# Encoder layer, output products: an earlier copy on ScalarE, a residual cut in two, two VectorE steps moved behind logits

## The chip, the cores and the metric

The kernel runs on one core of one Trainium2 chip. The metric is device time in microseconds of one execution; of a kernel several executions are timed and the median stands for it. In the profile PE is TensorE, PEld its weight loads, DVE is VectorE, ACT is ScalarE, POOL is GpSimd, and SP is SyncE, which here issues every DMA. Each engine takes its instructions strictly in the order in which the program holds them.

## The reference

One layer over 4096 tokens of 1024 channels, float32:

```
h = rmsnorm(x, pre_norm_g);  proj = h @ w_in                # 1024 -> 2304
q, k, v, g_a, u_p, g_p = split(proj)
a = banded_attention(q, k, v, rel_bias, sink) * silu(g_a)    # 8 heads of 64, 2 KV heads, |i-j| <= 128
p = multiscale_pool(u_p, pool_w, pool_scale) * silu(g_p)     # windows 2, 4, 8, 16
mixed = concat([a, p]) @ w_out                               # 1024 -> 1024
out = x + rmsnorm(mixed, post_norm_g)
```

`banded_attention` takes blocks of 128 queries against the block before, the same and the block after (384 keys). The softmax has a learned sink logit in its denominator. Every float32 operand of a product is carried as a pair of float16 (high and low part, three products for one).

## The kernel before, in words

The first half (to about 515 us) computes pooling, gates and the input projections and keeps some of them in DRAM. The second half, which alone is changed, goes backwards through 32 query blocks `b`, two of them (256 tokens) to a *unit* `u = b // 2`. For a unit it computes k, v and q, then for each block and each half of the heads (`visit(b, half)`) a softmax, then the attention values, and the output product.

A softmax is a chain over four engines: `scores` (PE, line 1272), four `logits` (DVE, line 1295), four `exps` (ACT, line 1306), `denominators` and a reciprocal (DVE, lines 1313 and 1316), four `probs` (ACT, line 1328: the high half `pn`), four `rests` (DVE, line 1336: the low half), and `turn` (SP, line 1345: one DMA that transposes all of it into `pt`). `values` (PE, line 1422) needs `pt` of both halves of a block; within a block it works through half 0 first and then half 1.

The output product of a unit is a 2x2 block product done in seven products instead of eight, named "11", "12", "22", "s1" to "s4" (12 matmuls each, line 1572). They share three PSUM banks 0 to 2 (`acc0` to `acc2`), and partial sums live in two SBUF tiles `mo[0]`, `mo[1]` of a unit (128x1024 float32, one buffer each for all units from 2 on, so unit `u` takes over the buffers of unit `u + 1`). The steps which the change touches:

- `mix_p1`: product "11" into bank 0; `begin` (ACT, line 1590, "COPY mo") copies bank 0 into the upper half of `mo[0]`.
- `mix_p6`: product "s2" into bank 1. `mix_p2`: product "12" is added on top in bank 0, so its first matmul must wait for `begin`. Then `square` (ACT, line 1595, "jkb") and `gain11` (DVE, line 1600) both read bank 0.
- `mix_p3`: product "s4"; it ends `mo[0]` of a unit: `mean` (DVE 1624, POOL 1629), `residual` (DVE, line 1633, "xr": `xr = mo * rs + xr`), `store` (SP, line 1639).

In the loop over odd blocks the order on PE is: "s4" of the unit before, k and v, `values(b+1)`, `scores(b, 1)`, then "22", "11", "s2", "12". The softmax of `(b, 1)` on DVE and ACT so runs beside these four products. The loop goes through this 13 times (units 14 to 2). The last units (2, 1 and 0) are written out one by one behind the loop, with `at_(t, step)`.

The order is a plan written by hand: `due(t, step)` puts a step into a list with a time `t`; the list is sorted by `t` and issued in that order, each engine receiving its own instructions. `t` is no time of the chip, it only sets the order. `pe(us, step)` moves PE's own planned clock on. Waits are set by a framework layer: by data, and a tile that takes over a buffer waits for the last reader of the tile before. Two readers of one PSUM bank on different engines are put one behind the other, in the order of the plan.

Of the kernel before, what the change touches and what calls it, by code (L numbers as in the profile page):

```python
# [19 lines left out]
D = 1024  # L20
# [19 lines left out]
O11, O12, O21, O22, OT1, OT2, OT4, OT3 = range(8)  # L40
# [94 lines left out]
def hybrid_layer(ctx: ExitStack, tc, io, out):  # L135
# [74 lines left out]
    with ExitStack() as actx:  # L210
# [689 lines left out]
        for j in range(4):  # L900
            ld(9.5 + 0.1 * j, wut[:, j], io["w_uT"][j], 0.5, w=[f"wut{j}"])
            z = turn("sq")
            for half in range(2):
                t = U0 + 4 * j + 2 * half
# [338 lines left out]
    def due(t, fn, *args):  # L1243
        plan.append((t, len(plan), fn, args))
# [283 lines left out]
    LO, HI = slice(0, 512), slice(512, D)  # L1528
# [123 lines left out]
    def pe(us, fn, *args):  # L1652

        due(now[0], fn, *args)
        now[0] += us
        return now[0]
# [27 lines left out]
    M = 2.6  # L1684

    def mix_p1(u):
        due(pe(M, product, u, "11", O11, 0) - 0.2, begin, u)

    def mix_p4(u):
        pe(M, product, u, "22", OT4, 2)  # L1690

    def mix_p2(u):
        t = pe(M, product, u, "12", O21, 0, True)
        due(t, square, u, 0, 0, 0)
        due(t + 0.1, gain11, u)

    def mix_p6(u):
        due(pe(M, product, u, "s2", OT2, 1), add, u, (0, HI), (0, HI), 1)
# [8 lines left out]
    def mix_p5(u):  # L1707
        t = pe(M, product, u, "s1", OT1, 1)
        due(t, add, u, (1, HI), (1, HI), 1)
        due(t + 0.7, square, u, 1, 1)  # L1710
        due(t + 1.4, gain, u, 1, HI)
        finish(u, 1, t + 4.0)

    def mix_p3(u):
        t = pe(M, product, u, "s4", O22, 1, True)
        due(t, add, u, (0, HI), (0, HI), 1)
        due(t + 0.7, square, u, 0, 1)
        due(t + 1.4, gain, u, 0, HI)
        finish(u, 0, t + 4.0, 6.4)

    def finish(u, i, t, late=0.0):

        due(t, mean, u, i)
        due(t + 2.0 + late, residual, u, i, slice(0, D))
        due(t + 3.4 + late, store, u, i, slice(0, D))

    u = NU - 1
# [10 lines left out]
    for b in reversed(range(2, NB)):  # L1740
        u = b // 2
# [13 lines left out]
        elif b == NB - 3:  # L1755
            due(free[1], load_wo, OT3)
            mix_p4(u + 1)
            mix_p1(u + 1)
            attend(b + 1, 1)
            visit(b, 1)  # L1760
            due(free[1], load_wo, OT1)
            due(free[1] + 8.0, load_wo, O22)
            do_kv(u - 1, 1)
            mix_p2(u + 1)
            mix_p6(u + 1)
        elif b % 2:
            mix_p3(u + 2)
            do_kv(u - 1)
            attend(b + 1, 0)
            visit(b, 1)  # L1770
            mix_p4(u + 1)
            mix_p1(u + 1)
            mix_p6(u + 1)
            mix_p2(u + 1)
        else:
            do_q(u - 1, 0, 2.0 * (b == NB - 2))
            if b < NB - 2:
                attend(b + 1, 0)
            visit(b, 1)
            do_q(u - 1, 1, 2.0 * (b == NB - 2), int(b < NB - 2))  # L1780
            due(now[0] + 2.1, load_x, u - 3)
            if b == NB - 2:
                attend(b + 1, 1)
            elif b > 2:
                mix_p7(u + 1)
                mix_p5(u + 1)
# [15 lines left out]
    def at_(t, fn, *args):  # L1802
        due(z + t, fn, *args)
# [11 lines left out]
    def cast(th, tw, u, name, f, eng):  # L1815
        at_(th, high, u, name, f)
        at_(tw, low, u, name, f, eng)

    def ending(u, i, tm, tr, split=False):
        at_(tm, mean, u, i)  # L1820
        for n, cs in enumerate((LO, HI) if split else (slice(0, D),)):
            at_(tr + 0.7 * n, residual, u, i, cs)
            at_(tr + 1.3 + 0.7 * n, store, u, i, cs)
# [39 lines left out]
    at_(12.3, square, 2, 0, 1)  # L1863
    at_(11.1, gain, 2, 1, LO, V)
    at_(11.8, gain, 2, 1, HI, V)
    ending(2, 1, 10.9, 12.5)
    at_(38.7, gain, 2, 0, HI, V)
    ending(2, 0, 13.8, 39.4)

# [7 lines left out]
    at_(16.55, sum4, 1)  # L1877
    cast(16.6, 18.9, 1, "s2", a11, V)
    cast(18.0, 18.1, 1, "s3", a21, G)
    at_(17.4, gain11, 1)  # L1880
    at_(17.8, square, 1, 0, 0, 0)
    cast(23.5, 24.2, 1, "s1", a_s1, V)
    at_(23.45, add, 1, (0, HI), (0, HI), 1)
# [115 lines left out]
```

## Time and profile before

| what | value |
|---|---|
| median of 3 runs | 1194.64 us (1194.54 to 1195.63) |
| the profiled execution | 1195.91 us, of which the span of its trace is 1194.10 us |
| PE busy | 1154.7 us, 97% of the span |
| DVE, ACT, POOL busy | 942.1, 702.1, 302.2 us |
| granted TensorE clock, mean | 0.996 |
| PE waiting for the copy of line 1590 | 6.7 us in 12 waits |

A timeline row reads: start (us from the span's start), duration, engine, line, operation, output<-inputs, shape, how many instructions were merged, and in brackets how long the engine sat idle before it and who released it. A row of waits reads: who waited, for whom, total us, number of waits, longest.

### The profile page before, as it was taken

How to read it: one execution, taken by the hardware profiler on the slowest of the kernel's cores; microseconds unless marked ns; L12 is line 12 of the kernel's file. 1: busy time of each engine (PE TensorE's matmuls, PEld its weight loads, DVE VectorE, ACT ScalarE, POOL GpSimd, SP SyncE). 2: the span in 40 equal slices, each digit the busy share in tenths (PEclk: the TensorE clock that was granted, in tenths of full speed). 3: DMA queues.
4: the chain of work that ended last, by engine and by line, in shares of the span. 5: the costliest groups of instructions: out<-in, count | busy, mean ns of one | idle time of the engine just before them, and what ended most of it. 6: DMA issues, size and time to landing. Idle time of an engine off the chain costs nothing. (4 is left out here: it accounts for less than half of the span.)

```text
span 1194.1 us, 33947 instructions
## 1 busy us (share of the span) xinstructions
PE 1154.7 (97%) x14304; PEld 884.4 (74%) x14304; DVE 942.1 (79%) x1866; ACT 702.1 (59%) x1459; POOL 302.2 (25%) x309
## 2 busy tenths in 40 slices
PE   5999999999999999898999999999999999999997
PEld 4998888988888888776667676576666667657643
DVE  6889996867888972567878877887887887788786
ACT  5865555645755541266565675666666567566662
POOL 0002111101101110203324433432542443343231
PEclk9999999999999999999999999999999999999999
DMA  8544587578657573487976876786786687686684
GB/s 315 209 124 151 168 280 242 171 238 261 217 174 251 164 203 109 135 229 177 255 177 139 201 185 128 198 196 164 173 188 177 136 204 187 133 187 164 162 233 124
DMA packets 292441, 224.65 MB, mean 188 GB/s; under 512 B 210704, under 2 KB 251920, under 8 KB 287680
## 3 DMA queue, kind: packets, MB, share of 16 engines
q1 hardware_dynamic: 292288, 222.48, 68.5%
q8 instruction: 112, 1.84, 0.6%
q14 instruction: 41, 0.34, 0.1%
HBM read 113.37 MB, written 60.33 MB: 145 GB/s over the span
## 5 line engine op out<-in xcount | busy, mean ns | idle before, releaser
L634 PEld LDWEIGHTS <-wq 128*128 128x128 f16 x4104 | 401.5, 98 | 52.8 <-issue 2.8
L634 PE MATMUL y<-xt,wq 128*128 128x256 f16 x1512 | 204.2, 273 | 0.9 <-ACT cc L742 0.9
L1336 DVE SCALAR_TENSOR_TENSOR pn<-p,rd,pn 128x384 f16<-128x384 f32 (+1 forms) x256 | 156.7, 654 | 30.5 <-ACT pn L1328 29.9
L1227 PE MATMUL aq<-xb,xb 128*128 128x256 f16 x1024 | 175.1, 275 | 0.0
L1306 ACT ACTIVATE p<-p,nm 128x385 f32<-128x385 f32 (+1 forms) x256 | 152.8, 599 | 33.5 <-DVE nm L1295 28.1
L1572 PE MATMUL ms<-wo,ys 128*128 128x512 f16 x720 | 163.1, 380 | 1.3 <-ACT pn L1328 0.9
L1295 DVE CUSTOM_DVE_ANT_0 p<-s,nt,nsink 128x384 f32<-128x384 f32 (+1 forms) x256 | 155.9, 665 | 1.5 <-PE s L1272 1.3
L1328 ACT ACTIVATE pn<-p,rd 128x384 f16<-128x384 f32 (+1 forms) x256 | 137.7, 598 | 30.7 <-issue 19.5
L1227 PEld LDWEIGHTS <-xb 128*128 128x128 f16 x1280 | 125.7, 98 | 23.7 <-issue 6.7
L1227 PE MATMUL aq<-xb,xt 128*128 128x256 f16 x512 | 140.5, 274 | 0.0
L1572 PEld LDWEIGHTS <-ys 128*128 128x128 f16 x720 | 69.0, 98 | 83.4 <-issue 3.4
L1572 PE MATMUL m<-wo,y 128*128 128x512 f16 x540 | 121.8, 380 | 7.8 <-ACT mo L1590 6.7
L304 POOL TENSOR_TENSOR yt<-yt,sg 128x512 f32<-128x512 f32 (+2 forms) x32 | 48.0, 1499 | 311.4 <-DVE yt L307 300.8
L1572 PEld LDWEIGHTS <-y 128*128 128x128 f16 x540 | 51.4, 98 | 73.2 <-issue 13.1
L1606 POOL TENSOR_TENSOR mo<-mo,gpost 128x512 f32<-128x512 f32 x39 | 63.8, 1636 | 92.9 <-ACT jkb L1595 91.7
L634 PE MATMUL plain<-xb,wq 128*128 128x256 f16 x576 | 68.8, 277 | 3.0 <-ACT xb L446 1.8
L1272 PE MATMUL s<-k_all,q 64*32 64x288 f16 (+8 forms) x3648 | 63.7, 268 | 6.9 <-ACT q L1216 3.9
L1227 PEld LDWEIGHTS <-xt 128*128 128x128 f16 x640 | 62.9, 98 | 8.7
L634 PE MATMUL y<-xb,wq 128*128 128x256 f16 x504 | 68.9, 273 | 0.0
L634 PE MATMUL v<-xb,wq 128*128 128x256 f16 x504 | 68.6, 273 | 0.2 <-DVE cc L304 0.2
L634 PE MATMUL v<-xt,wq 128*128 128x256 f16 x504 | 68.6, 273 | 0.0
L634 PE MATMUL x<-xb,wq 128*128 128x256 f16 x504 | 68.3, 273 | 0.0
(211 smaller groups left out, 1912.2 us busy)
## 6 DMA issues: line engine op xcount, KB each, us to landing
nt<-in_xT SPq DMA_DIRECT2D x28, 512.0 KB, 4.8
x_scr<-xb SPq DMA_DIRECT2D x14, 1024.0 KB, 7.2
xb<-x_scr SPq DMA_DIRECT2D x14, 1024.0 KB, 7.5
xr<-in_x SPq DMA_DIRECT2D x28, 512.0 KB, 4.5
out<-xr SPq DMA_DIRECT2D x28, 512.0 KB, 2.6
xn<-in_x SPq DMA_DIRECT2D x27, 512.0 KB, 4.5
ga_scr<-cc SPq DMA_DIRECT2D x64, 128.0 KB, 2.1
raw<-in_w_out SPq DMA_DIRECT2D x16, 512.0 KB, 5.3
```

Source lines behind the costliest of these rows:

```text
L304: eng.tensor_tensor(out=out, in0=in0, in1=in1, op=op)
L634: nc.tensor.matmul(b[:, s], wq[:, slot[q, op], wv, s, k, :], x[:, xv, k, :], start=(first and k + s + wv + xv == 0), stop=(last and k == H ...
L1227: nc.tensor.matmul(acc, w[:, j, k, :], x[:, kh, v, kt, :], start=(n == 0), stop=(n == 3 * KT - 1),)
L1272: nc.tensor.matmul(s_ps[qs, gg, c0:c1], q_t[u, half][a, qi, jj, tl + 32 * hq : tl + 32 * hq + 32], k_all[a, ki, kc + c0 - s0 : kc + c1 - s ...
L1295: nc.vector.tensor_tensor_reduce(out=p_t[b, half][:, hh, :nk], in0=s_t[jj][:, gg, :nk], in1=bias[:, h, lo : lo + nk], scale=negc[:, h : h ...
L1306: nc.scalar.activation(p[:, hh, : nk + 1], p[:, hh, : nk + 1], AF.Exp, bias=nm_t[b, half][:, hh : hh + 1], scale=-1.0, accum_out=den_t[b, ...
L1328: nc.scalar.activation(prob_view(b, half)[:, 0, i], p_t[b, half][:, i, :nk], AF.Copy, scale=rd_t[b, half][:, i : i + 1],)
L1336: nc.vector.scalar_tensor_tensor(out=pn4[:, 1, i], in0=p_t[b, half][:, i, :nk], scalar=rd_t[b, half][:, i : i + 1], in1=pn4[:, 0, i], op0= ...
L1572: nc.tensor.matmul(z_t[u, tag], y[:, k, yi, :], wo[o][:, wi, k, :], start=(n == 0 and acc is None), stop=(n == 3 * HK - 1), skip_group_che ...
L1606: eng.tensor_tensor(out=mo, in0=mo, in1=gpost[:, cs], op=ALU.mult)
```

## The change

Four edits to the plan, and no change to what is computed. `begin` is due 0.8 earlier. In `mix_p2`, `gain11` comes first and `square` 0.1 behind it. The residual that `mix_p3` ends with is issued as two halves of 512 channels, with the store still one. Among the written-out last units, the residual of block 4 (unit 2, `i = 1`; its store with it) and `gain11` of unit 1 come later.

```
     def mix_p1(u):
-        due(pe(M, product, u, "11", O11, 0) - 0.2, begin, u)
+        due(pe(M, product, u, "11", O11, 0) - 1.0, begin, u)
...
         t = pe(M, product, u, "12", O21, 0, True)
-        due(t, square, u, 0, 0, 0)
-        due(t + 0.1, gain11, u)
+        due(t, gain11, u)
+        due(t + 0.1, square, u, 0, 0, 0)
...
         due(t + 1.4, gain, u, 0, HI)
-        finish(u, 0, t + 4.0, 6.4)
+        due(t + 4.0, mean, u, 0)
+        due(t + 12.4, residual, u, 0, LO)
+        due(t + 13.1, residual, u, 0, HI)
+        due(t + 13.8, store, u, 0, slice(0, D))
...
-    ending(2, 1, 10.9, 12.5)
+    ending(2, 1, 10.9, 19.2)
...
-    at_(17.4, gain11, 1)
+    at_(19.1, gain11, 1)
```

`finish` loses its argument `late`, which no other call used; its planned times are the same as before.

ACT's order at the copy, unit 9, before (`p`, `den`: exponentials; `pn`: probabilities; `m_9`: PSUM bank 0; `ys`, `jkb`: operands and squares of the output product):

```order
L1306 ACTIVATE p_1_11951,den_1_11949<-p_1_11951,nm_1_11948 128x385 [waits DVE_49] x3
L1328 ACTIVATE pn_1_11980<-p_1_11951,rd_1_11950 128x384 [waits DMAHW4_49,DVE_49,Activation_49]
L1590 COPY mo_0_11983<-m_9_11963 128x512 [waits PE_49]
L1328 ACTIVATE pn_1_11980<-p_1_11951,rd_1_11950 128x384 [waits Activation_49]
L1328 ACTIVATE pn_1_11980<-p_1_11951,rd_1_11950 128x384
L1328 ACTIVATE pn_1_11980<-p_1_11951,rd_1_11950 128x384 [waits Activation_49]
L1474 CAST ys_9_12025<-at_11880 128x4x128
L1474 CAST ys_9_12027<-s_9_11931 128x4x128 [waits PE_49]
L1595 ACTIVATE jkb_00_12030,ss_11985<-m_9_11963 128x512
```

And now:

```order
L1306 ACTIVATE p_1_11956,den_1_11954<-p_1_11956,nm_1_11953 128x385 [waits DVE_49] x3
L1590 COPY mo_0_11983<-m_9_11968 128x512 [waits DVE_49,PE_49]
L1328 ACTIVATE pn_1_11989<-p_1_11956,rd_1_11955 128x384 [waits DMAHW4_49,Activation_49]
L1328 ACTIVATE pn_1_11989<-p_1_11956,rd_1_11955 128x384 [waits Activation_49]
L1328 ACTIVATE pn_1_11989<-p_1_11956,rd_1_11955 128x384
L1328 ACTIVATE pn_1_11989<-p_1_11956,rd_1_11955 128x384 [waits Activation_49]
L1474 CAST ys_9_12031<-at_11885 128x4x128
L1474 CAST ys_9_12033<-s_9_11936 128x4x128 [waits PE_49]
L1595 ACTIVATE jkb_00_12133,ss_11985<-m_9_11968 128x512 [waits DVE_49]
```

The copy moved one place, ahead of the first of the four probabilities, and now names a wait for DVE itself: the instruction waited for is the second half of the residual, the last reader of the buffer which `mo[0]` takes over. The square now waits for DVE too, which is `gain11`.

DVE's order at the same place, unit 9, before (ISA: a logits instruction; `xr`: the residual of the unit before):

```order
L1295 ISA p_1_11951,nm_1_11948<-s_5947,nt,nsink,negc 128x384
L1295 ISA nm_1_11948 128x1
L1633 SCALAR_TENSOR_TENSOR xr_11499<-mo_0_11190,rs_0_11788,xr_11499 128x1024 [waits DMAHW3_49,DMAHW1_49,Pool_49]
L1313 TENSOR_SCALAR den_1_11949<-den_1_11949 128x4 [waits Activation_49]
L1316 RECIPROCAL rd_1_11950<-den_1_11949 128x4 [waits DVE_49]
L1336 SCALAR_TENSOR_TENSOR pn_1_11980<-p_1_11951,rd_1_11950,pn_1_11980 128x384 [waits DMAHW4_49,Activation_49]
L1336 SCALAR_TENSOR_TENSOR pn_1_11980<-p_1_11951,rd_1_11950,pn_1_11980 128x384 [waits Activation_49] x3
L1611 TENSOR_TENSOR mo_0_11983<-ms_9_11989,mo_0_11983 128x512 [waits PE_49]
L1600 TENSOR_TENSOR mo_0_11983<-m_9_11963,gpost 128x512 [waits Activation_49]
```

And now:

```order
L1295 ISA p_1_11956,nm_1_11953<-s_5947,nt,nsink,negc 128x384
L1295 ISA nm_1_11953 128x1
L1633 SCALAR_TENSOR_TENSOR xr_11504<-mo_0_11189,rs_0_11793,xr_11504 128x512 [waits DMAHW3_49,DMAHW1_49,Pool_49]
L1313 TENSOR_SCALAR den_1_11954<-den_1_11954 128x4 [waits Activation_49]
L1316 RECIPROCAL rd_1_11955<-den_1_11954 128x4 [waits DVE_49]
L1633 SCALAR_TENSOR_TENSOR xr_11504<-mo_0_11189,rs_0_11793,xr_11504 128x512
L1336 SCALAR_TENSOR_TENSOR pn_1_11989<-p_1_11956,rd_1_11955,pn_1_11989 128x384 [waits DMAHW4_49,DVE_49,Activation_49]
L1336 SCALAR_TENSOR_TENSOR pn_1_11989<-p_1_11956,rd_1_11955,pn_1_11989 128x384 [waits Activation_49] x3
L1611 TENSOR_TENSOR mo_0_11983<-ms_9_11995,mo_0_11983 128x512 [waits DVE_49,PE_49]
L1600 TENSOR_TENSOR mo_0_11983<-m_9_11968,gpost 128x512 [waits PE_49]
```

The residual's second half now stands behind the reciprocal, and `gain11` (line 1600) waits for PE's product "12", where it waited for ACT's square. Its place in the row is the same. This holds for all 13 units of the loop.

DVE's order among the last units, softmax of block 1, half 1, before (`xb<-m_1`: `gain11` of unit 1; `ys_1<-at`: the low part of operand "s2"). The residual of block 4 stood seven instructions ahead of these rows, just ahead of the `gate` of block 2:

```order
L1295 ISA p_1_18618,nm_1_18615<-s_5946,nt,nsink,negc 128x384
L1295 ISA nm_1_18615 128x1
L1600 TENSOR_TENSOR xb_68<-m_1_18407,gpost 128x512 [waits PE_49]
L1295 ISA p_1_18618,nm_1_18615<-s_5947,nt,nsink,negc 128x384
L1295 ISA nm_1_18615 128x1
L1295 ISA p_1_18618,nm_1_18615<-s_5947,nt,nsink,negc 128x384
L1295 ISA nm_1_18615 128x1
L1478 TENSOR_TENSOR ys_1_18622<-at_18171,ys_1_18622 128x4x128 [waits Activation_49]
L1313 TENSOR_SCALAR den_1_18616<-den_1_18616 128x4 [waits Activation_49]
```

And now:

```order
L1295 ISA p_1_18629,nm_1_18626<-s_5947,nt,nsink,negc 128x384
L1295 ISA nm_1_18626 128x1
L1478 TENSOR_TENSOR ys_1_18633<-at_18184,ys_1_18633 128x4x128 [waits Activation_49]
L1600 TENSOR_TENSOR xb_68<-m_1_18420,gpost 128x512 [waits Activation_49]
L1633 SCALAR_TENSOR_TENSOR xr_18237<-mo_1_17925,rs_1_18472,xr_18237 128x1024 [waits DMAHW7_49,Pool_49]
L1313 TENSOR_SCALAR den_1_18627<-den_1_18627 128x4 [waits Activation_49]
```

Both steps now stand between the last logits and the denominators. On SP the store of block 4 moved behind the loads of a gate, of a pooling operand and of a weight, to just ahead of the transpose of block 1, half 1. On PE and POOL nothing moved.

More of the change, by code (lines that the diff above doesn't have):

```diff
@@ L1718, in mix_p3, with finish @@
         due(t + 1.4, gain, u, 0, HI)
-        finish(u, 0, t + 4.0, 6.4)
-    def finish(u, i, t, late=0.0):
+        due(t + 4.0, mean, u, 0)
+        due(t + 12.4, residual, u, 0, LO)
+        due(t + 13.1, residual, u, 0, HI)
+        due(t + 13.8, store, u, 0, slice(0, D))
+    def finish(u, i, t):
         due(t, mean, u, i)
-        due(t + 2.0 + late, residual, u, i, slice(0, D))
-        due(t + 3.4 + late, store, u, i, slice(0, D))
+        due(t + 2.0, residual, u, i, slice(0, D))
+        due(t + 3.4, store, u, i, slice(0, D))
     u = NU - 1
```

## The prediction

> **What bounds the kernel now.** I read the page first, then the waits of PE, then the timeline of each engine around the longest of them.
>
> ```profile
> span 1194.1 us, 33947 instructions
> PE 1154.7 (97%) x14304; PEld 884.4 (74%) x14304; DVE 942.1 (79%) x1866; ACT 702.1 (59%) x1459; POOL 302.2 (25%) x309
> PEclk9999999999999999999999999999999999999999
> ```
>
> PE is the bound, at a granted clock in the top tenth throughout. Only its idle time can be won, so I ask what PE waits for. From 640 us on, and (third row) between 500 and 640 us:
>
> ```profile
> PE m L1572 <- ACT mo L1590: 6.0, 11, 0.6
> PE s L1272 <- DVE nm L1295: 1.1, 1, 1.1
> PE m L1572 <- ACT mo L1590: 0.7, 1, 0.7
> ```
>
> The copy costs PE 6.7 us in 12 listed waits; the loop runs 13 times, and I count 13. The second row is one wait among the last units. Both are what the change touches. One pass (unit 9) on PE, ACT, DVE and POOL:
>
> ```profile
> 810.39 2.75 PE L1572 MATMUL ms<-wo,ys 128*128 128x512 f16 x12
> 813.72 2.75 PE L1572 MATMUL m<-wo,y 128*128 128x512 f16 x12 [0.58 <-ACT mo L1590]
> 810.51 0.60 ACT L1306 ACTIVATE p<-p,nm 128x385 f32<-128x385 f32 x1
> 812.59 0.62 ACT L1328 ACTIVATE pn<-p,rd 128x384 f16<-128x384 f32 x1 [1.38 <-issue]
> 813.11 0.56 ACT L1590 COPY mo<-m 128x512 f32<-128x512 f32 x1
> 813.57 1.63 ACT L1328 ACTIVATE pn<-p,rd 128x384 f16<-128x384 f32 x3
> 810.32 1.89 DVE L1633 SCALAR_TENSOR_TENSOR xr<-mo,rs,xr 128x1024 f32<-128x1024 f32 x1
> 812.13 0.16 DVE L1313 TENSOR_SCALAR den<-den 128x4 f32<-128x4 f32 x1
> 812.33 0.18 DVE L1316 RECIPROCAL rd<-den 128x4 f32<-128x4 f32 x1
> 817.75 0.69 DVE L1600 TENSOR_TENSOR mo<-m,gpost 128x512 f32<-128x512 f32 x1 [1.25 <-ACT jkb L1595]
> 809.86 1.28 POOL L1516 TENSOR_TENSOR yf<-yf,at 128x512 f32<-128x512 f32 x1
> ```
>
> Product "s2" ends at 813.14 and "12" starts at 813.72, 0.61 after the copy started. The copy's data was there long before, since "11" stands ahead of "s2" on PE. It starts late because it stands behind the first probability, which waits for the reciprocal (ends 812.51), which stands on DVE behind the residual.
>
> **The change part by part, against the profiled execution (1195.91 us: span 1194.10 and 1.81 around it; the median, 1194.64, is 1.27 lower).**
>
> *The copy.* ACT is idle from about 811.2 (the exponential above, 0.60, and its accumulator read) to 812.59. If the copy could run there, "12" would follow "s2" at once: the listed 0.58 would go. But the copy now waits for the residual's second half, which is behind the reciprocal. When does that end? Rows for the durations of a residual and of a half, and for what may follow a reciprocal:
>
> ```profile
> 798.75 1.28 DVE L1633 SCALAR_TENSOR_TENSOR xr<-mo,rs,xr 128x1024 f32<-128x1024 f32 x1 [0.36 <-POOL rs L1629]
> 798.81 2.36 POOL L1606 TENSOR_TENSOR mo<-mo,gpost 128x512 f32<-128x512 f32 x1
> 1184.57 0.75 DVE L1633 SCALAR_TENSOR_TENSOR xb<-xb,rs,xb 128x512 f32<-128x512 f32 x1
> 1168.84 0.18 DVE L1316 RECIPROCAL rd<-den 128x4 f32<-128x4 f32 x1
> 1168.93 0.66 DVE L1611 TENSOR_TENSOR xb<-ms,xb 128x512 f32<-128x512 f32 x1
> ```
>
> Undisturbed, a residual takes 1.28. At 810.32 it took 0.61 more, beside a POOL instruction begun 0.46 earlier; at 798.75 it began 0.06 before POOL and POOL was the one that paid (2.36). So the later of the two is held, and here the first half pays the 0.61: 0.75 + 0.61, and, since the next instruction starts 0.08 before the listed end (812.13 against 812.21), the denominators start at 810.32 + 1.28 = 811.60. Reciprocal at 811.80 (0.20 behind, as before), second half at 811.90 (0.09 behind a reciprocal, last two rows), end 812.65, copy at 812.73 (ACT followed DVE by 0.08 before: 812.51 to 812.59). "12" then starts at 812.73 + 0.61 = 813.34: **0.38 earlier**, a third of the wait left. The bounds: nothing (the second half held as well), and 0.58.
>
> *The Trainium skill on that hold.* The page "SBUF — State Buffer", section "SBUF: two separate sides", says that the port pair of VectorE and GpSimd is an exclusive lock for a whole instruction, and that a VectorE instruction with two SBUF inputs blocks fully against it. By that the sum would be the one of the third rival below. The trace agrees on who pays, but not in full: blocked to POOL's end at 811.14, the residual of before would have ended at 812.42, and it ended at 812.21.
>
> *The probabilities behind the copy.* The first starts at 812.73 + 0.46 = 813.19 instead of 812.59, the last at 814.73 instead of 814.59, since the copy is no longer between them. The rests end, and the transpose is issued, 0.14 later, while PE comes 0.38 earlier. What waits for the transpose is the second half of the next `values`:
>
> ```profile
> 815.96 3.64 SPq L1345 DMA_TRANSPOSE pt<-pn  x1
> DMA to landing us min/median/max: 7.2/7.2/7.2
> DMA to landing us min/median/max: 5.5/5.5/5.5
> DMA to landing us min/median/max: 5.4/7.0/8.2
> 822.80 0.25 PE L1422 MATMUL o<-pt,vv 128*64 128x128 f16 x2
> 865.61 0.25 PE L1422 MATMUL o<-pt,vv 128*64 128x128 f16 x2
> 866.31 0.22 PE L1422 MATMUL o<-pt,vv 128*64 128x128 f16 x2
> ```
>
> The second half starts 0.70 after the first (last two rows), in unit 9 at 823.50. The second and third rows are the slowest and fastest of the nine such transposes whose landing is on record, the fourth is that of all transposes from 640 to 1120 us. Afterwards: issue at 816.10, use at 823.12, so it must land within 7.02. Up to 7.2 in these nine: up to 0.18 lost, 0 in most. In the pass around 865.61 (issue at 858.97, landing 7.2, so 0.14 to spare) 0.38 would be lost. I take 0.07 as a mean. **Per unit 0.38 - 0.07 = 0.31, 13 units: 4.0 us.**
>
> *`gain11` ahead of `square`* costs no instruction. `gain11` loses its 1.25 us wait for ACT, so the next logits start about 0.8 earlier against PE; the square waits for `gain11`, about 0.5 us, ahead of a cast and of exponentials that the earlier logits have room for. PE waits for neither: zero on the path. If that cover were missing, the next softmax would be 0.5 later, and its transpose, issued at 826.63, is used from 845.42 on:
>
> ```profile
> 826.63 3.60 SPq L1345 DMA_TRANSPOSE pt<-pn  x1
> 845.42 0.25 PE L1422 MATMUL o<-pt,vv 128*64 128x128 f16 x2
> ```
>
> *The second half's own cost*, 2 x 0.75 - 1.28 = 0.22 us on DVE, is in the sum above. The store still waits for both halves, with the transpose behind it on SP only at 816.
>
> *The last units.* DVE takes the residual of block 4 and `gain11` out of the way of block 1's logits:
>
> ```profile
> 1143.12 1.28 DVE L1633 SCALAR_TENSOR_TENSOR xr<-mo,rs,xr 128x1024 f32<-128x1024 f32 x1
> 1144.32 0.48 DVE L1446 SCALAR_TENSOR_TENSOR at<-o,gaf,gb 128x256 f32<-128x256 f32 x1
> 1149.73 0.67 DVE L1295 CUSTOM_DVE_ANT_0 p<-s,nt,nsink 128x384 f32<-128x384 f32 x1
> 1151.18 1.16 POOL L1478 TENSOR_TENSOR ys<-at,ys 128x512 f16<-128x512 f32 x1 [2.34 <-ACT ys L1474]
> 1152.35 0.17 DVE L1313 TENSOR_SCALAR den<-den 128x4 f32<-128x4 f32 x1 [1.33 <-ACT p L1306]
> 1155.86 0.68 DVE L1611 TENSOR_TENSOR xb<-ms,xb 128x512 f32<-128x512 f32 x1
> 1150.47 0.52 PE L1272 MATMUL s<-k_all,q 64*32 64x160 f16 x24 [1.14 <-DVE nm L1295]
> 1156.60 1.64 PE L1572 MATMUL ms<-wo,ys 128*128 128x512 f16 x6 [0.32 <-DVE xb L1611]
> ```
>
> The gate moves from 1144.32 to about 1142.95 (1.37), the last logits by a further 0.60 to 1147.77: PE's 1.14 goes. But PE's next wait (0.32, for DVE's add at 1155.86) comes later in the same chain, and DVE now has the 0.68 and the 1.28 between logits and denominators. `gain11` would start near 1149.0 and the residual near 1149.6, which is when POOL's row of 1151.18 would also start, moved forward by the same chain. If the residual is first, the denominators start at about 1150.85, 1.5 earlier than 1152.35; if POOL is first, the residual is held and they start at about 1151.8, 0.55 earlier. PE's gain at the add is that of the denominators: 0.55 to 1.5. I take the middle, **1.0 us**. The store comes 5 us later but ahead of its transpose, which moves forward itself; behind it all is one chain that shifts as a whole.
>
> **Sum: 4.0 + 1.0 = 5.0 us**, 1195.91 - 5.0 = 1190.9 for a profiled execution, 1189.6 for the median.
>
> **Rivals.**
> - *The wait goes entirely.* If the hold on the first half is shorter than 0.61, or its POOL instruction moves, the copy is early enough: 13 x 0.58 + 1.5 = 9.0, 1185.6. For it: ACT is idle from 811.2. Against: 0.3 us would have to come from somewhere.
> - *The transposes take the wait's place.* The 0.14 that the transpose comes later, and 0.4 us of spare time in passes with a landing of 7.0 to 7.2, leave nothing of the loop's gain if landings shift to about 7.4; the last units alone give 1.0: 1193.6. Against: three of nine landed in 6.1 or less.
> - *The first half is held to POOL's end* (809.86 + 1.28 = 811.14) and then takes its 0.75, to 811.89 instead of 811.68: 0.21 off the 0.38 leaves 0.17 per unit, 2.2 for 13, and 0.55 at the end: 2.8, 1191.9. Against: by the same hold the residual of before would end 0.21 after its row.
> - *Slower.* The same transposes, landing after 8.2 (the longest of any, row above): use at 816.10 + 8.2 = 824.30 instead of 823.50, 0.80 lost per unit, 10.4 - 1.0 = 9.4 us, 1204.0. It decides from a landing of 7.4 (no gain) or 7.7 (measurably slower); the slowest of its kind was 7.2.
>
> **Chances.** Forecast 0.62, wait gone entirely 0.12, transposes 0.13, first half held to the end 0.08, slower 0.05. A measurement here tells about 0.2%, 2.4 us, from no change. Faster: 0.62 + 0.12 + 0.08 = 0.82; within it: 0.13; slower: 0.05. The range goes from 1185.4 (the first rival included) to 1192.2 (the third included), and leaves out the transposes and the slower case.
>
> **What would show it.** Right: the copy starts about 0.4 earlier relative to product "s2" and directly after a 512-wide residual; the wait of line 1572 for line 1590 falls from 0.58 to about 0.2; `gain11` no longer waits for ACT; the 1.14 of line 1272 is gone and the wait at the add grows. Wrong: a wait of line 1422 for `pt` in most units (the transposes), no wait for line 1590 at all (the hold is shorter), or an unchanged wait (the second half was held too).

## The result: 2.9 us faster, where 5.0 were forecast

| | before | after |
|---|---|---|
| median of 13 runs each | 1195.63 us | 1192.38 us |
| ratio | | 0.9976 (95% interval 0.9968 to 0.9985) |
| the profiled execution and its span | 1195.91, 1194.1 us | 1192.04, 1190.3 us |
| loop, 13 passes | 553.45 us | 551.40 us |
| from the end of the loop to the end of the span | 73.32 us | 72.77 us |

By the ratio, which is that of the means, the change is worth 2.9 us (1.8 to 3.8), or 0.24%; the medians are 3.25 apart. The loop is measured from the first values step after unit 15's copy to that after unit 2's, by the start of these rows. Timeline of PE, kernel before:

```profile
567.31 0.25 PE L1422 MATMUL o<-pt,vv 128*64 128x128 f16 x2
1120.76 0.25 PE L1422 MATMUL o<-pt,vv 128*64 128x128 f16 x2
1122.68 0.93 PE L1272 MATMUL s<-k_all,q 64*32 64x288 f16 x48
```

And kernel after:

```profile
566.09 0.25 PE L1422 MATMUL o<-pt,vv 128*64 128x128 f16 x2
1117.49 0.25 PE L1422 MATMUL o<-pt,vv 128*64 128x128 f16 x2
1119.72 0.93 PE L1272 MATMUL s<-k_all,q 64*32 64x288 f16 x48
```

The third row of each is the `scores` step behind the values step that ends the loop; it is needed further below.

The spans differ by 3.8 us, of which 1.22 (567.31 to 566.09) lie ahead of the loop, where nothing was changed. 2.05 came from the loop and 0.55 from the last units: 2.6 in all, against 2.9 by the times. The page after:

```profile
span 1190.3 us, 33985 instructions
PE 1154.4 (97%) x14304; PEld 884.8 (74%) x14304; DVE 941.9 (79%) x1879; ACT 703.8 (59%) x1459; POOL 303.4 (25%) x309
```

PE has the same work; what fell is its idle time. The waits of PE in the loop of the kernel after (560 to 1120 us; who waited, for whom, total, times, longest):

```profile
PE m L1572 <- ACT mo L1590: 1.7, 9, 0.2
PE aq L1227 <- DVE q L1217: 1.6, 7, 0.6
PE s L1272 <- issue: 1.0, 1, 1.0
PE o L1422 <- DMA pt<-pn: 0.2, 1, 0.2
```

And behind it (1120 to 1195 us):

```profile
PE ms L1572 <- DVE xb L1611: 0.8, 1, 0.8
PE m L1572 <- DVE mo L1611: 0.4, 1, 0.4
```

The wait for the copy went from 6.7 us to 1.7, or from 0.58 to about 0.2 a pass, as forecast. The second row is new. PE projects the queries of a unit in two parts; the second part takes over PSUM bank 1 from the first and waits until DVE has read the first part's sums out of it (line 1217, `q`). PE stands for that in 7 of 13 passes. The prediction has no such wait. One pass (unit 10), PE, DVE, ACT and POOL:

```profile
767.03 2.75 PE L1572 MATMUL ms<-wo,ys 128*128 128x512 f16 x12
769.98 2.75 PE L1572 MATMUL m<-wo,y 128*128 128x512 f16 x12 [0.19 <-ACT mo L1590]
781.89 0.27 PE L1227 MATMUL aq<-xb,xb 128*128 128x256 f16 x1 [0.18 <-DVE q L1217]
766.96 1.35 DVE L1633 SCALAR_TENSOR_TENSOR xr<-mo,rs,xr 128x512 f32<-128x512 f32 x1
768.24 0.16 DVE L1313 TENSOR_SCALAR den<-den 128x4 f32<-128x4 f32 x1
768.53 0.72 DVE L1633 SCALAR_TENSOR_TENSOR xr<-mo,rs,xr 128x512 f32<-128x512 f32 x1
773.20 0.68 DVE L1600 TENSOR_TENSOR mo<-m,gpost 128x512 f32<-128x512 f32 x1
781.14 0.69 DVE L1217 SCALAR_TENSOR_TENSOR q<-aq,q 128x512 f16<-128x512 f32 x1 [0.37 <-ACT q L1216]
769.34 0.59 ACT L1590 COPY mo<-m 128x512 f32<-128x512 f32 x1 [1.49 <-DVE xr L1633]
773.91 0.60 ACT L1595 ACTIVATE jkb<-m 128x512 bf16<-128x512 f32 x1 [0.53 <-DVE mo L1600]
774.50 0.61 ACT L1474 CAST ys<-yf 128x512 f16<-128x512 f32 x1
775.18 1.16 POOL L1478 TENSOR_TENSOR ys<-yf,ys 128x512 f16<-128x512 f32 x1 [0.36 <-ACT ys L1474]
776.28 0.31 POOL L1289 COPY p<-nsink 128x4 f32<-128x4 f32 x2
776.51 0.62 ACT L1306 ACTIVATE p<-p,nm 128x385 f32<-128x385 f32 x1 [1.40 <-POOL p L1289]
780.54 0.57 ACT L1216 ACTIVATE q<-aq 128x512 f16<-128x512 f32 x1
```

The rows of the copy's own chain fall where the prediction placed them: first half 1.35 long, denominators 1.28 behind its start, second half 1.57, copy 2.38 (forecast 1.36, 1.28, 1.58, 2.41), and "12" starts 2.95 behind "s2" where it was 3.33 (813.72 - 810.39): 0.38 earlier, the forecast to the hundredth. That it fits so closely is in part chance: the copy started 0.03 sooner than forecast, and "12" 0.64 behind it instead of 0.61.

Read the lower part from line 1600 on. The square (line 1595) stands idle 0.53 for `gain11`. The cast of line 1474 behind it is that much later, so is POOL's low part, and POOL's small copy of the sink logits into `p` (line 1289) stands behind that low part in POOL's queue. The exponentials of the next softmax take that logit in as the 385th column of `p`, and wait for the copy. They start 776.51 - 769.98 = 6.53 behind "12". Here are the same rows in the kernel before, in unit 9 (POOL twice, ACT, DVE; "12" started at 813.72):

```profile
818.32 1.16 POOL L1478 TENSOR_TENSOR ys<-yf,ys 128x512 f16<-128x512 f32 x1
819.42 0.31 POOL L1289 COPY p<-nsink 128x4 f32<-128x4 f32 x2
819.65 0.62 ACT L1306 ACTIVATE p<-p,nm 128x385 f32<-128x385 f32 x1 [1.42 <-DVE nm L1295]
824.28 0.69 DVE L1217 SCALAR_TENSOR_TENSOR q<-aq,q 128x512 f16<-128x512 f32 x1 [0.37 <-ACT q L1216]
```

There it is 5.93. The exponentials start 0.23 behind the start of the sink copy in both kernels, although the row of before names DVE as the releaser. Behind the exponentials stand two probabilities and then `q` (lines 1216 and 1217), so DVE's `q` begins 11.16 behind "12", where it was 10.56. Against "s2" that is 14.11 and 13.89: `q` comes 0.22 later in the pass, while PE comes 0.38 sooner and finds the bank not yet read.

### The profile page after: what moved, and what is told of

Read it like the earlier page. It is cut to its first block, busy times and chain, and to the rows that moved or that the text cites. A ratio compares the mean times of both kernels' runs of the same rounds, so it can differ in the third digit from the quotient of the medians.

```text
span 1190.3 us, 33985 instructions
## 1 busy us (share of the span) xinstructions
PE 1154.4 (97%) x14304; PEld 884.8 (74%) x14304; DVE 941.9 (79%) x1879; ACT 703.8 (59%) x1459; POOL 303.4 (25%) x309
## 5 line engine op out<-in xcount | busy, mean ns | idle before, releaser
L1272 PE MATMUL s<-k_all,q 64*32 64x288 f16 (+7 forms) x3648 | 62.9, 266 | 5.9 <-ACT q L1216 3.6
```

Of the source, the lines that this page charges most:

```text
L1272: nc.tensor.matmul(s_ps[qs, gg, c0:c1], q_t[u, half][a, qi, jj, tl + 32 * hq : tl + 32 * hq + 32], k_all[a, ki, kc + c0 - s0 : kc + c1 - s ...
```

## The experiments

The theory was: the swap of `gain11` and `square` delays the next softmax through POOL's sink copy, and PE pays at `q`. Its rivals: the split of the residual is what costs, since it sends the copy behind a reciprocal; the later transposes cost; or the part of the last units carries more or less than was forecast. e1 to e4 ran on one chip (kernel before: 1194.47), e5 to e7 on another (1195.10). Loop and end are measured as in the table above. In all nine profiles one `scores` row near 677 us stands between 0.7 and 1.3 us for a reason that the profile does not name, so a difference of half a microsecond between two loops says nothing.

| run | median us | ratio (95%) | loop us | end us |
|---|---|---|---|---|
| e1, square first | 1189.99 | 0.9962 (0.9947 to 0.9977) | 548.87 | 72.87 |
| e2, residual whole | 1187.18 | 0.9935 (0.992 to 0.995) | 546.67 | 72.75 |
| e3, last units only | 1194.72 | 1.0001 (0.9991 to 1.001) | 553.29 | 72.71 |
| e4, sink copy early | 1189.70 | 0.9960 (0.9946 to 0.9974) | 549.40 | 72.80 |
| e5, e1 and e2 together | 1186.14 | 0.9929 (0.9916 to 0.9941) | 545.12 | 72.82 |
| e6, copy's place alone | 1187.60 | 0.9934 (0.992 to 0.9947) | 545.04 | 73.30 |
| e7, e2 and e4 together | 1185.93 | 0.9922 (0.9909 to 0.9936) | 545.05 | 72.72 |

**e1: the swap undone.**

```
-        due(t, gain11, u)
-        due(t + 0.1, square, u, 0, 0, 0)
+        due(t, square, u, 0, 0, 0)
+        due(t + 0.1, gain11, u)
```

> The changed kernel with one edit undone: in mix_p2 square stands ahead of gain11 again. The loop's stretch (from the values step behind unit 15's copy to that behind unit 2's, 13 passes) was 553.45 us before and 551.40 after, 2.05 us instead of the 4.0 forecast, and a new wait of 0.18 us has come up on PE: projection q waits for VectorE's q (line 1217). Theory A (the swap costs): the square waits for gain11, the cast behind it on ScalarE and GpSimd's low part come later, and GpSimd's copy of the sink logit behind them holds the next exponentials; undone, the exponentials start 0.6 us earlier against product 12 (5.93 us behind its start instead of 6.53), the wait for q is gone, and the stretch falls by up to 13 x 0.18 = 2.3 us, to 549.1 to 550.5. Theory B (PE only catches up with a chain whose place the swap doesn't set): the wait for q stays at 0.1 to 0.2 and the stretch at 551.4 +- 0.4. Theory C (the swap helps, as earlier logits): the stretch gets longer, to 552 or more.

The loop went to 548.87, 2.53 less than after. One pass of e1 (timeline; PE, POOL, ACT):

```profile
768.78 2.75 PE L1572 MATMUL m<-wo,y 128*128 128x512 f16 x12 [0.20 <-ACT mo L1590]
774.68 0.32 POOL L1289 COPY p<-nsink 128x4 f32<-128x4 f32 x2
774.91 0.62 ACT L1306 ACTIVATE p<-p,nm 128x385 f32<-128x385 f32 x1 [1.63 <-POOL p L1289]
```

Its longest row of PE's waits in the loop:

```profile
PE m L1572 <- ACT mo L1590: 2.1, 10, 0.3
```

The exponentials start 6.13 behind "12", 0.40 sooner than in the kernel after (5.93 was expected), and PE no longer waits for `q`. The loop is a little shorter than expected. The copy's wait is still about 0.2. So the swap took 2.5 us of the loop's gain. What is left, 553.45 - 548.87 = 4.58, is 0.35 a pass: close to the 0.38 that the prediction had for the copy. That leaves little for the transposes.

**e4: the sink copy ahead of the low part, the swap kept.** This cuts the chain at another place. If the theory is right, the square may go on waiting for `gain11`.

```
+    def sink(b, half):
...
     def softmax(b, half, t):
+        if b % 2 == 0 and half == 0:
+            due(t - 3.0, sink, b, half)
```

> The changed kernel with GpSimd's copy of the sink logit (line 1289 before) for each even block's first half placed ahead of the three low parts, where GpSimd is idle for 4.7 us. Theory A: this copy is what releases the exponentials; they start as soon as ScalarE is through with the cast, about 1.2 us earlier (5.2 us behind the start of product 12 instead of 6.53), the wait for q is gone, and the stretch falls by up to 2.3 us, to 549.1 to 550.5. Rival (the logits or ScalarE hold the exponentials, the copy is only the last in line): the exponentials move by less than 0.3 us, the wait for q stays and the stretch is 551.4 +- 0.4.

The new `sink` holds the allocation of `p` and the sink copy, taken out of `logits`. Its added lines shift the numbers, so that 1572 reads 1579, 1595 reads 1602 and 1306 reads 1311. Timeline of PE and ACT:

```profile
767.58 2.75 PE L1579 MATMUL m<-wo,y 128*128 128x512 f16 x12 [0.20 <-ACT mo L1597]
771.51 0.60 ACT L1602 ACTIVATE jkb<-m 128x512 bf16<-128x512 f32 x1 [0.53 <-DVE mo L1607]
772.61 0.62 ACT L1311 ACTIVATE p<-p,nm 128x385 f32<-128x385 f32 x1
```

PE's waits for the copy in the loop:

```profile
PE m L1579 <- ACT mo L1597: 2.1, 10, 0.3
```

The square still stands 0.53 for `gain11`. But the exponentials now start 5.03 behind "12", with no idle time ahead of them, and the wait for `q` is gone. The loop is 549.40, 2.0 less than after. So the square's wait costs through POOL's queue; that is shown from two sides. Of the 2.5 us, 0.5 does not come back here. That is no more than the unnamed wait near 677 us, which was 1.3 here and 0.8 in e1, and with the residual whole nothing is left of it (e7 against e5, below). The intervals of e1 and e4 overlap with that of the kernel after, so the price of the swap rests on the loops of the traces, one for each kernel, and not on the times.

**e2: the residual in one piece again, at the same place.**

```
-        due(t + 12.4, residual, u, 0, LO)
-        due(t + 13.1, residual, u, 0, HI)
+        due(t + 12.4, residual, u, 0, slice(0, D))
```

> The changed kernel with the residual of mix_p3 in one piece again. If the copy waits for the end of the residual (the second half, behind the reciprocal), it can start 0.4 us earlier without the split: about 2.0 us behind the residual's start instead of 2.38, and PE's wait for it (0.19) is gone; the probabilities, the rests, gain11, the square and what follows come 0.4 us earlier as well, so the wait for q shrinks to under 0.1, and the stretch falls by 0.25 to 0.35 a pass, to 547 to 548.5. Rival: the split earns something, since the denominators come 0.6 us later without it; then the exponentials' chain gets later, a wait for pt or q grows, and the stretch is 551.4 or more.

The loop went to 546.67, 4.73 less than after, and below the range expected. Timeline of PE, DVE and ACT in one pass:

```profile
765.53 2.75 PE L1572 MATMUL ms<-wo,ys 128*128 128x512 f16 x12
768.12 2.75 PE L1572 MATMUL m<-wo,y 128*128 128x512 f16 x12
765.47 1.90 DVE L1633 SCALAR_TENSOR_TENSOR xr<-mo,rs,xr 128x1024 f32<-128x1024 f32 x1
767.46 0.59 ACT L1590 COPY mo<-m 128x512 f32<-128x512 f32 x1 [1.10 <-DVE den L1313]
```

The longest row of PE's waits in the loop:

```profile
PE aq L1227 <- DVE q L1217: 1.2, 5, 0.6
```

The residual is held just as before (1.90), and still the copy starts 767.46 - 765.47 = 1.99 behind the residual's start, directly behind its end. With two halves it was 2.38: the copy waits for the second half, which stands behind denominators and reciprocal. The row names the denominators as the releaser, but they stand behind the residual and the copy starts 0.09 behind the residual's listed end, as it did behind the second half's. The wait for `q`, expected under 0.1, stayed at 0.15 to 0.19 in four passes and 0.55 in one. "12" has no wait at all here. It starts 2.59 behind "s2"; so the time that PE lost at this place was 3.33 - 2.59 = 0.74 before and 2.95 - 2.59 = 0.36 after, each some 0.17 more than the idle time in brackets.

**e3: the last units alone, on the kernel before.**

```
-    ending(2, 1, 10.9, 12.5)
+    ending(2, 1, 10.9, 19.2)
...
-    at_(17.4, gain11, 1)
+    at_(19.1, gain11, 1)
```

> The kernel before with only the two steps of the last units moved (residual of block 4 and gain11 of unit 1 behind the logits). Both theories of the loop expect its stretch unchanged at 553.4 +- 0.3. The forecast had 1.0 us for this part; the trace of the changed kernel shows 0.87 (from the start of block 1's second scores to the last product s1). Expected 0.6 to 1.5 us: 1.5 if VectorE's residual takes the port ahead of GpSimd's low part, 0.55 to 0.9 if GpSimd is first.

The end went from 73.32 to 72.71, and the times (1.0001, interval 0.9991 to 1.001) cannot tell it from nothing. All the kernels with this edit end in 72.71 to 72.87, those without it (before, e6) in 73.30 and 73.32: 0.43 to 0.61 us, where 1.0 was forecast.

**e5, e6, e7: what each loop edit is worth.** e5 is the kernel after with the edits of e1 and e2, e7 with those of e2 and e4. e6 is the kernel before with the copy's due time alone:

```
-        due(pe(M, product, u, "11", O11, 0) - 0.2, begin, u)
+        due(pe(M, product, u, "11", O11, 0) - 1.0, begin, u)
```

> The changed kernel with both undone: residual in one piece and square ahead of gain11; what is left of the change is the earlier copy and the two steps of the last units. Theory A (the square held by gain11 delays GpSimd's sink copy, this the exponentials, these q) and the copy waiting for the residual's end: both of the waits that the changed kernel shows are gone (0.19 for the copy, 0.18 for q), product 12 follows s2 directly, and the stretch is that of the whole residual, 546.67, less its waits for q (1.5 in all): 545.2 +- 0.6, 8.2 us under the kernel before. Rival (the transposes become the bound now that PE is 0.6 to 0.7 earlier a pass): waits for pt of 0.1 to 0.4 in most passes and a stretch of 547 or more.

> The kernel before with one edit only: begin due 0.8 earlier. If the copy's place alone carries the loop's gain, the stretch is that of the whole residual with square first: 545.2 +- 0.6, and the time behind the loop is that of the kernel before (73.3 +- 0.2 us from the last values step of the stretch to the end; 72.8 with the last units' steps moved). Rival (the other edits are needed for it): a stretch of 549 or more.

> The changed kernel with the residual in one piece and the sink copy early, gain11 still ahead of square. Theory A: with the sink copy out of the way the order of gain11 and square does not matter to PE: no wait for q, stretch 545.2 +- 0.6 as with square first. Rival (gain11 first costs PE by itself): the wait for q stays at 0.13 to 0.19 in several passes and the stretch at 546.3 or more.

All three loops take 545.04 to 545.12. PE's waits in the loop of e5:

```profile
PE s L1272 <- issue: 1.1, 1, 1.1
PE o L1422 <- DMA pt<-pn: 0.2, 1, 0.2
```

The end of its loop, which began at 566.09 (timeline of PE):

```profile
1111.21 0.25 PE L1422 MATMUL o<-pt,vv 128*64 128x128 f16 x2
```

Neither the copy nor `q` holds PE any longer, and the one listed wait for `pt`, at 1112.28, lies behind the loop's end. So the copy's new place alone brings 553.45 - 545.04 = 8.4 us. Beside it the split costs 3.75 (548.87 - 545.12), and the swap 1.55 without the split (546.67 - 545.12) or 2.53 with it. Together, 545.12 + 3.75 + 2.53 = 551.40, the loop after. By their ratios to the kernel before, e2, e5, e6 and e7 (0.9922 to 0.9935) are faster than the kernel after (0.9976), clear of the intervals; among the four the intervals overlap.

## Why the prediction fell short

**The step that failed: "`gain11` ahead of `square` costs no instruction ... zero on the path."** It named the wait of 0.5 correctly (0.53) and the exponentials behind it, but followed the delay on ACT and DVE only. It missed that the same cast releases POOL's low part, and that the exponentials' own `p` is begun by a POOL copy behind that low part. Its fallback, a transpose issued 18.8 us ahead of its use, was sound, but PE needs `q` sooner than that transpose, and `q` stands behind the exponentials on ACT as well. Priced by e1: 2.53 us where the sum had nothing, more than the whole gap between 2.05 in the loop and the 4.0 forecast for it.

PE's starts over the 13 passes, kernel after against before, show the same. From "s2" to "12" it gained 4.92; from `scores` to the projection of the queries it lost 2.17; in the values steps 0.54; in the unnamed wait near 677 us 0.30. With 0.14 gained in small differences that makes the 2.05.

**The copy: right for the kernel as changed.** The hold on the first half, the denominators, the second half and the copy came out within 0.03 us of their working, and over the loop it gained 4.92, where 13 x 0.38 is 4.94, though not evenly: 0.71 in the first pass, nothing in the third, which had no wait before. What the prediction did not ask is whether the split, which it listed as 0.22 us of DVE, delays the copy against a whole residual. It does, by 0.39 (2.38 against 1.99), and that is worth 3.75 us (e1 against e5), more than all that was measured. The row for it stood in its own fence: the residual of before ended at 812.21, ahead of the reciprocal.

**The transposes: 0.07 a pass was about right.** The profile lists one wait for `pt` in the loop, 0.2 us. Start to start shows more: from its first row to the `scores` behind it a values step takes 1.92 when nothing holds it, as at 1120.76 before. In the kernel after it took 2.24, 2.09 and 2.35 in three steps of the loop and 2.23 in the one that ends it (1117.49 to 1119.72), each time with the second half's rows late; in the kernel before, 2.30 in one. So it lost 1.23 against 0.38: 0.85 more, where 13 x 0.07 = 0.9 was forecast. That the unlisted ones too waited for `pt` is read from their place. The rival in which the transposes take the wait's place fell: in e5, in which PE loses 0.74 a pass less at the copy, they cost 0.6 in all.

**"The wait goes entirely"** can be had (e5, e6, e7), but not as that rival put it, by a shorter hold on the first half. The hold stayed; the way is not to split. It also undersized the prize: 13 x 0.58 is 7.5, and 8.4 was there. By the starts of "s2" and "12" most passes lost 0.74 and not the 0.58 of the brackets, two lost 0.55 and one nothing: 8.7 in all.

**The last units: the mechanism was right, the size in the lower part of its range.** The 1.14 of line 1272 is gone, and the wait at the add grew from 0.32 to 0.79. POOL was first by 0.01, the residual was held, and the denominators started 0.58 earlier against block 1's second `scores` (3.54 behind them before, 2.96 after), as in the lower of the two cases (0.55). From these `scores` to "s1" PE took 7.79 before, 7.21 in e3 and 6.92 after: 0.58 and 0.87 gained. The table's 0.55 for the kernel after is less, since the 0.31 that the values step of 1117.49 lost is counted behind the loop. But the upper case, 1.5, did not exist. Timeline of POOL and DVE, kernel after:

```profile
1146.66 1.16 POOL L1478 TENSOR_TENSOR ys<-at,ys 128x512 f16<-128x512 f32 x1 [2.08 <-ACT ys L1474]
1146.67 2.23 DVE L1633 SCALAR_TENSOR_TENSOR xr<-mo,rs,xr 128x1024 f32<-128x1024 f32 x1
1148.82 0.16 DVE L1313 TENSOR_SCALAR den<-den 128x4 f32<-128x4 f32 x1
1149.01 0.18 DVE L1316 RECIPROCAL rd<-den 128x4 f32<-128x4 f32 x1
```

And in e2, where the residual was first:

```profile
1141.87 1.27 DVE L1633 SCALAR_TENSOR_TENSOR xr<-mo,rs,xr 128x1024 f32<-128x1024 f32 x1
1142.02 2.14 POOL L1478 TENSOR_TENSOR ys<-at,ys 128x512 f16<-128x512 f32 x1 [2.25 <-ACT ys L1474]
1143.19 1.00 DVE L1313 TENSOR_SCALAR den<-den 128x4 f32<-128x4 f32 x1
1144.22 0.18 DVE L1316 RECIPROCAL rd<-den 128x4 f32<-128x4 f32 x1
```

Whoever is first, the reciprocal starts 2.34 or 2.35 behind the start of the residual. With POOL first, the residual takes 2.23. With the residual first, POOL is held, and then the denominators take 1.00 instead of 0.16, up to POOL's end at 1144.16. The order of the two moves the hold from one DVE instruction to the next and saves nothing.

**What chance did to the number.** The third rival (first half held to POOL's end) had 2.8 us, nearer to the 2.9 than the forecast's 5.0, but what it describes did not happen: by it the first half would have taken 1.57 and the copy won 0.17 a pass, and it took 1.35 and won 0.38. And the kernel before took 1195.63 in these runs, 1.0 more than the 1194.64 from which the forecast counts. Without that the measured time would not lie 0.2 above the forecast's upper bound of 1192.2: as a gain, that bound is 2.4 us. The error of the sum is the same either way.

## What to carry to other kernels

When a step is made to wait, follow every engine that its output feeds, down to small setup instructions that stand behind the delayed work in another queue: here an instruction of 0.2 us on POOL carried 0.4 of the square's 0.5 us of delay into the next softmax. When an edit makes something earlier by cutting a piece of work in two, price it against the piece left whole, since a consumer that needs both parts gets the last one later. And ask of each part of a change whether it is needed: one due time alone was worth 8.4 us of the loop, and its two companions gave 6.3 of it back.

## What the runs showed beyond that

- The price of a wait on PE is larger than the idle time in brackets: 0.58 listed and 0.74 from start to start, 0.19 and 0.36. The difference stayed near 0.17. A product of 12 matmuls is listed with 2.75, but an undisturbed pair starts 2.59 apart, so start-to-start distances are the better measure. They also show waits that the profile does not list, as in the values steps.
- VectorE and GpSimd hold each other for nearly the whole of an instruction: beside POOL's 1.16 the residual grew by 0.95 (2.23 against 1.28), and POOL's by 0.98 beside the residual. The Trainium skill, page "SBUF — State Buffer", section "SBUF: two separate sides", calls it an exclusive lock for a whole instruction. These rows fall as far short of that as those of the kernel before: held to POOL's end at 1147.82 the residual would have taken 2.43, 0.20 more than it did. In e2 the denominators behind the residual, a step of 128x4 with one input, took 1.00 instead of 0.16, up to POOL's end; that the same hold did it is read from the ends, no run took POOL's instruction away.
- A named releaser can be the wrong one: the row of before that names DVE's `nm` was held by POOL's sink copy, as the same 0.23 behind it in the kernel after, and e4, show.
- The first half of the program, equal in these kernels, did not end at the same time in each profile: the first copy of `begin` started at 545.16 before, 543.94 after, 543.41 in e3 and 542.35 in e4. A difference of spans of that size says nothing on a change. It goes with the granted clock: from 500 to 515 us its mean was 0.77 before, 0.89 after and in e3, and 1.00 in e4, and 1.00 in each of them from there to the loop's end. The page's row of the clock, in slices of 30 us, shows a 9 throughout and hides it.
